# Two-layer hybrid decoder trunk: a re-planned start, three accumulator banks, joined PV groups and a split last output piece

## Chip, core and metric

The kernel runs on one core of a Trainium2 chip. The metric is the device time of one execution in microseconds (us), here the median of three runs. The profile is one further execution, with its own time.

## What is computed

`x` is 256 tokens by 1024 columns, float32. Layer 0 normalises it, projects it once, and splits the columns between a Mamba-2 SSD mixer and a dilated attention mixer of 24 heads; layer 1 is a causal attention of 16 heads. Cut to what matters here:

```python
# layer 0
proj = rms_norm(x, norm_w) @ w_in              # 1024 -> 8208 columns: z, xbc, dt, q, k, v, g
xs, B, C = split(silu(causal_dwconv(xbc)))     # conv of 4 taps per column
y = ssd(xs, softplus(dt + bias), -exp(a_log), B, C) + d_skip * xs
y = rms_norm_per_group(y * silu(z))
q, k = rope(rms_norm(q)), rope(rms_norm(k))    # per head, 24 heads of 64
o = merge_by_softmax([attention(q, k, v, window, dilation) for 3 groups]) * silu(g)
x = x + concat(y, o) @ w_out                   # 1536 -> 1024
# layer 1: with 256 tokens the one block of 256 makes it plain causal attention
q, k, v, g = split(rms_norm(x) @ w_in1)        # 4 x 1024 columns, 16 heads of 64
x = x + (causal_attention(rope(rms_norm(q)), rope(rms_norm(k)), v) * silu(g)) @ w_out1
```

## The kernel before

All weights are brought as 58 tiles of 128 x 2048 float32 (1 MB) in the order of use. `load_split` (line 576) loads a tile in two DMAs of 512 KB into `raw`; ScalarE casts each half to fp32r (`whi`, line 591) and VectorE takes the difference (`wlo`, line 592). Each product of activations and weights is three matmuls (`mm3`, line 667, and `proj_fm`): high by high, high by low, low by high. `raw`, `whi` and `wlo` have three buffers each, so a tile is prepared two ahead of its use.

The first projections (`q2`, `v0`, `k01_0`) read the transposed input `xt_host` (`load_xf`, line 1212, tile names `k` and `mix`), the later ones `xh` and `xl`, which `normalise` (line 1234) writes from the same data once the row norms (`rms`, line 631) are known. Ten matmuls on zeros warm TensorE first (line 1205). One `for` over `ORDER0`, then the output projection (`out_proj`, line 725), then `ORDER1`, then the second `out_proj`, whose `finish` is `store` (line 1319): two halves of 256 columns are added and written out for each piece.

PSUM has eight banks: two under the tag `acc` for projections and six under `x` for everything else (line 566): score tiles, transposes (`x<-cst,...`, `cst` holding the identity), PV sums and broadcasts. Score matmuls (`x<-qkT,qkT`) use 64 of 128 rows and PV matmuls (`x<-p,k`) 64 of 128 columns; two of them run side by side in the halves of the array. `plan.group()` keeps the matmuls of one such group together.

Nothing is issued as it is written. Every call is recorded (`record`, line 240), and `Plan.order` (line 343) lays the recorded operations out on the five engines by a list schedule: among the operations that a table of costs (`price`, line 286) holds to be ready, the one recorded first goes first, buffers being given out as they come free. `choose` (line 445) stays in a half-array shape while it can. `emit` (line 497) then issues all of it; so every profile row has line L504. A changed number in `price`, another count of banks or another position in the recording re-lays the whole program.

Of the kernel before, what the change touches and what calls it, by code (L numbers as in the profile page):

```python
# [20 lines left out]
S = 256  # L21
# [14 lines left out]
NWARM = 10  # L36
# [149 lines left out]
class Plan:  # L186
# [15 lines left out]
    def __init__(self, nc, sbuf, psum):  # L202
        self.nc, self.sbuf, self.psum = nc, sbuf, psum
        self.ops, self.tags, self.groups = [], {}, []
        for e in self.ENGINES:
            setattr(self, e, Recorder(self, e))
# [31 lines left out]


    def record(self, engine, method, args, kw):  # L240
# [45 lines left out]
    def price(self, op, outs, ins):  # L286
# [8 lines left out]
        if e == "pe":  # L295
# [4 lines left out]
            elif lhs.dtype == F32R:  # L300
                c = max(119.5, 0.453 * n + 5)
# [41 lines left out]
    def order(self):  # L343
# [8 lines left out]
        for op in ops:  # L352
            op.left = len(op.preds)
            op.ready = 0.0
            for p in op.preds:
                ops[p].succs.append(op.seq)
# [6 lines left out]
        for op in ops:  # L363
            if not op.left:
                heapq.heappush(waiting[op.engine], (0.0, op.seq))
# [180 lines left out]
def trunk_kernel(ctx: ExitStack, tc: tile.TileContext, x, tiles_host, dtw_host, norms, xt_host, params, bparams, consts, causal_mask, out):  # L546
# [18 lines left out]
    def pst(tag, shape=(P, 512)):  # L565
        tag, bufs = ("acc", 2) if tag == "acc" else ("x", 6)
# [9 lines left out]
    def load_split(between=()):  # L576
# [4 lines left out]
        for h in range(2):  # L581
            sl = slice(1024 * h, 1024 * h + 1024)
# [5 lines left out]
        step = 1024 // n  # L588
        for k in range(0, nk, step):
            sl = slice(k, k + step)  # L590
# [134 lines left out]
    def out_proj(mix, parts, finish, by_column=()):  # L725

        accs, nk = {}, len(mix)
        for k0, n in parts:
# [3 lines left out]
            def run(t, c, k):  # L732
# [4 lines left out]
                mm3(accs[t, c], (h[:, ts_], l[:, ts_]), (wh[:, kk, :], wl[:, kk, :]), k == 0, k == nk - 1)  # L737

            if not last:
                for c in range(2):  # L740
                    for i in range(n // 4):
                        w[c, i] = weights()
                        for t in range(NT):
                            if k0 + i == 0:
                                accs[t, c] = pst("o" if (t, c) == (1, 1) else "acc")
                            for k in range(4):
                                run(t, c, k0 + 4 * i + k)
            else:
                w = {(c, 0): weights() for c in range(2)}
                for t in range(NT):  # L750
                    steps = [(c, k) for k in range(k0, nk) for c in range(2)]
                    for c, k in sorted(steps) if t in by_column else steps:
                        run(t, c, k)
                        if k == nk - 1:
                            finish(t, c, accs[t, c])

# [34 lines left out]
    def small_params():  # L791
        rows = sb([NROWS, P], name="rows")
        sp.dma_start(rows, params)
        tp = pst("t")
        pe.transpose(tp[:, :NROWS], rows, ident[:NROWS, :NROWS])
        dve.tensor_copy(pc, tp[:, :NROWS])
        sp.dma_start(bp, bass.AP(bparams.tensor, bparams.offset, [[0, P], [1, 160]]))
# [18 lines left out]
    def dt_path():  # L816
        sp.dma_start(flat(dtw), dtw_host)
# [226 lines left out]
    def pv(op, pTs, vs, first, last, dilated=False):  # L1044

        with plan.group():
            for kt, (c0, n, l0) in enumerate(((0, 128, 0), (128, 128, 0)) if dilated else ((0, 256, 0), (256, 128, 128))):
                for j in range(2):
                    o = op[64 * j:64 * j + 64, :]
                    o = blocks(o)[:, kt] if dilated else o[:, l0:l0 + n]  # L1050
                    pe.matmul(o, vs[j][kt], pTs[j][:, c0:c0 + n], start=first and kt == 0, stop=last and kt == 1)
# [75 lines left out]
    def dil_pair(pr):  # L1127
        def fn():
            op = pst("o")
            for g in range(3):  # L1130
# [4 lines left out]
                pv(op[:, :S], pTs, vs, g == 0, g == 2, g > 0)  # L1135
# [71 lines left out]
    dve.memset(all1, 1.0)  # L1207
    sp.dma_start(ncol, norms)
# [10 lines left out]
    load_split([lambda: load_xf(1)])  # L1219
    load_xf(2)  # L1220
    load_split([lambda: load_xf(3)])
    sp.dma_start(ident, consts[:, IDN:IDN + P])
    load_split()
    for t in range(NT):
        load_x(t)
    first, normal = Rows(lambda k: entry[k]), Rows(lambda k: (xh[:, k, :], xl[:, k, :]))
# [17 lines left out]
    def switch(n):  # L1244
        if n == FIRST - 2:
            normalise()
        if n == FIRST - 1:
# [55 lines left out]
    def pairs1(c):  # L1303
        def fn():
            for j in range(0, 8, 2):
# [3 lines left out]
                pv(op[:, :S], pTs, [[state[f"V{c}"][t][:, j + i, :] for t in range(NT)] for i in range(2)], True, True)  # L1309
# [9 lines left out]
    def store(t, c, acc):  # L1319
        for h in range(2):  # L1320
            sl = slice(256 * h, 256 * h + 256)
            dve.tensor_tensor(xt[t, c][:, sl], xt[t, c][:, sl], acc[:, sl], ALU.add)
# [42 lines left out]
```

## Time and profile before

| | us |
|---|---|
| median of 3 runs (lowest, highest) | 410.09 (409.61, 410.75) |
| profiled execution, its own time | 411.14 |
| its span, first to last instruction | 409.4 |
| TensorE busy in the span | 399.6 |
| VectorE busy | 319.7 |
| ScalarE busy | 258.3 |
| GpSimd busy | 58.2 |

A row of the timeline gives the start in us, the time it covers, engine, operation, the tiles as out<-in, the shape, and in brackets the idle time before it with what ended that. PE is the matmul side of TensorE. A float32 matmul stands as two records, an fp32r one as one; records overlap, since the next matmul starts while one drains, so the distance of starts is the time that a matmul takes up.

### The profile page before, as it was taken

Reading aid. Unit: us, or ns where it says so; the run is one execution under the profiler, and the core shown is the slowest. Engines: PE = TensorE matmul, PEld = TensorE weight load, DVE = VectorE, ACT = ScalarE, POOL = GpSimd, SP = SyncE. Lnnn points to the kernel's source line nnn. Section 1 sums busy time; section 2 is a strip of 40 time slices with the busy share of each in tenths; the row PEclk is TensorE's granted clock in tenths of the full one; section 3 lists DMA queues with packets and bytes.
Section 4 is the critical chain, followed back from the end, with each engine's and each line's share of the span. In section 5 each row is a group of like instructions: output and inputs, shape, how many; then the busy total and the mean of one; then the engine's idle time right before and its main releaser. Section 6 shows DMA issues by size and latency. Waiting matters only on the chain.

```text
span 409.4 us, 7018 instructions
## 1 busy us (share of the span) xinstructions
PE 399.6 (98%) x2511; PEld 339.2 (83%) x2511; DVE 319.7 (78%) x809; ACT 258.3 (63%) x530; POOL 58.2 (14%) x65
## 2 busy tenths in 40 slices
PE   5999999999999999999999999999999999999996
PEld 5878999999889677778889888888878978879784
DVE  3788999999679999999948794597589756698532
ACT  4778666466356696568677963586569646586610
POOL 0080310000022000334004000002430004500000
PEclk9899999999999999999999999999999999999999
DMA  7997565556636235545518344264741734543002
GB/s 232 379 357 258 193 227 178 163 179 199 203 108 255 96 114 189 171 161 165 165 59 287 117 155 155 83 228 149 251 163 54 252 98 156 177 142 102 2 26 77
DMA packets 22994, 68.82 MB, mean 168 GB/s; under 512 B 4163, under 2 KB 5936, under 8 KB 22960
## 3 DMA queue, kind: packets, MB, share of 16 engines
q1 hardware_dynamic: 22960, 68.39, 50.5%
q8 instruction: 19, 0.31, 0.3%
q14 instruction: 15, 0.12, 0.1%
HBM read 67.28 MB, written 1.10 MB: 167 GB/s over the span
## 4 chain that ended last, share of the span: by engine, by line
PE 87%; DVE 7%; DMA 3%; POOL 1%; ACT 1%; issue 0%; SPq 0%; DVEq 0%
PE acc L504 69%; PE x L504 18%; DVE p L504 3%; DVE wlo L504 2%; DMA raw<-in_tiles_dram 1%; DMA qkT<-cd 1%; DVE k L504 1%; POOL ysq L504 1%; ACT k L504 1%; SPq L504 0%; ACT whi L504 0%; DVE t L504 0%; DVE rq L504 0%; POOL rq L504 0%; DVEq L1361 0%
## 5 line engine op out<-in xcount | busy, mean ns | idle before, releaser
L504 DVE TENSOR_TENSOR wlo<-raw,whi 128x1024 fp32r<-128x1024 f32 x116 | 139.7, 1219 | 24.8 <-ACT whi L504 23.9
L504 ACT CAST whi<-raw 128x1024 fp32r<-128x1024 f32 x116 | 119.5, 1050 | 31.8 <-PE acc L504 21.1
L504 PE MATMUL acc<-xh,whi 128*128 128x256 f32 x288 | 80.4, 279 | 0.0
L504 PE MATMUL acc<-xh,wlo 128*128 128x256 f32 x288 | 80.2, 278 | 0.0
L504 PE MATMUL acc<-xl,whi 128*128 128x256 f32 x288 | 79.9, 277 | 0.0
L504 PE MATMUL acc<-whi,xh 128*128 128x512 f32 x192 | 77.8, 405 | 0.0
L504 PE MATMUL acc<-wlo,xh 128*128 128x512 f32 x192 | 76.5, 399 | 0.0
L504 PE MATMUL acc<-whi,xl 128*128 128x512 f32 x192 | 76.5, 399 | 0.0
L504 PE MATMUL acc<-whi,mix 128*128 128x512 f32 x216 | 70.9, 403 | 2.9 <-ACT whi L504 2.3
L504 PEld LDWEIGHTS acc<-xh,whi 128*128 128x128 f32 x288 | 54.1, 188 | 0.7 <-issue 0.5
L504 PEld LDWEIGHTS acc<-xh,wlo 128*128 128x128 f32 x288 | 54.2, 188 | 0.3 <-issue 0.2
L504 PEld LDWEIGHTS acc<-xl,whi 128*128 128x128 f32 x288 | 54.1, 188 | 0.2
L504 PEld LDWEIGHTS acc<-whi,mix 128*128 128x128 f32 x216 | 41.1, 191 | 12.5 <-ACT whi L504 2.5
L504 PE MATMUL acc<-wlo,mix 128*128 128x512 f32 x108 | 43.1, 401 | 0.5 <-DVE wlo L504 0.5
L504 PEld LDWEIGHTS acc<-whi,xh 128*128 128x128 f32 x192 | 36.3, 189 | 8.6 <-issue 1.5
L504 PEld LDWEIGHTS acc<-wlo,xh 128*128 128x128 f32 x192 | 36.3, 189 | 8.5 <-issue 1.6
L504 PEld LDWEIGHTS acc<-whi,xl 128*128 128x128 f32 x192 | 36.3, 189 | 7.3 <-issue 0.2
L504 POOL TENSOR_TENSOR rq<-rq,nhalf 128x8 f32<-128x8 f32 x20 | 40.1, 2011 | 1.4
L504 ACT COPY k<-acc 128x512 f32<-128x512 f32 x24 | 14.1, 586 | 29.4 <-PE acc L504 29.4
L504 ACT ACTIVATE k<-k 128x512 f32<-128x512 f32 x20 | 12.7, 636 | 21.4 <-DVE k L504 21.4
L504 PEld LDWEIGHTS acc<-wlo,mix 128*128 128x128 f32 x108 | 20.7, 192 | 5.1 <-DVE wlo L504 1.0
L504 DVE TENSOR_REDUCE rq<-k 128x8 f32<-128x512 f32 x20 | 13.6, 682 | 11.5 <-ACT k L504 11.3
(150 smaller groups left out, 541.4 us busy)
## 6 DMA issues: line engine op xcount, KB each, us to landing
raw<-in_tiles_dram SPq DMA_DIRECT2D x116, 512.0 KB, 4.8
k<-in_x_dram SPq DMA_DIRECT2D x8, 256.0 KB, 6.4
qkT<-cd SPq DMA_DIRECT2D x4, 512.0 KB, 4.7
k<-in_xt_dram SPq DMA_DIRECT2D x4, 256.0 KB, 6.8
out_dram<-k SPq DMA_DIRECT2D x8, 128.0 KB, 1.8
cst<-in_consts_dram SPq DMA_DIRECT2D x1, 640.0 KB, 5.7
cst<-in_causal_mask_dram SPq DMA_DIRECT2D x1, 192.0 KB, 3.1
cst<-in_consts_dram SPq DMA_DIRECT2D x2, 64.0 KB, 5.8
```

The costliest lines, as they stand in the source:

```text
L504: getattr(eng[op.engine], op.method)(*[real(a) for a in op.args], **{k: real(v) for k, v in op.kw.items()})
```

## The change

The first weight tile is loaded and prepared in pieces of 512, 512 and 1024 columns; a small activation on ScalarE loads its table at the start; eleven warming matmuls instead of ten. The parameter rows, the rope tables and `bp` are loaded directly behind the first three tiles, and two weight tiles more are recorded ahead of the loads of `x`; those, `dtw` and the large constants get an earliest planning time. Three `acc` banks and five `x` banks. The PV matmuls of the three dilation groups of a head pair form one group. The last piece of the second output projection has two accumulators of 256 columns. The planner's price of an fp32r matmul changes.

```diff
-NWARM = 10
+NWARM = 11
@@ Plan
+    def later(self, n):        # recorded priorities inside are put back by n
+    def not_before(self, ns):  # operations inside are not planned ahead of ns
...
-        op.prio = op.seq
+        op.prio = op.seq + self.delay
+        op.ready = self.earliest
...
-                c = max(119.5, 0.453 * n + 5)
+                c = max(114.5, 0.447 * n)
@@ pst
-        tag, bufs = ("acc", 2) if tag == "acc" else ("x", 6)
+        tag, bufs = ("acc", 3) if tag == "acc" else ("x", 5)
@@ load_split
-        for h in range(2):
-            sl = slice(1024 * h, 1024 * h + 1024)
+        pieces = (512, 512, 1024) if i == 0 else (1024, 1024)
+        c = 0
+        for size in pieces:
+            sl = slice(c, c + size)
+            c += size
             sp.dma_start(flat(raw)[:, sl], tiles_host[i, :, sl])
...
-        step = 1024 // n
-        for k in range(0, nk, step):
-            sl = slice(k, k + step)
+        k = 0
+        for size in pieces:
+            sl = slice(k, k + size // n)
+            k += size // n
             act.copy(hi[:, sl, :], raw[:, sl, :])
@@ out_proj(mix, parts, finish, by_column=(), halves=False)
+                            split_up = halves and (t, c) == (NT - 1, 1)
+                                if split_up:
+                                    half_accs += [pst("o", (P, 256)) for _ in range(2)]
...
+                for hf in range(2 if halves else 0):
+                    for k in range(k0, nk):
+                        run_halves(k, hf)       # run(...) on 256 columns of the weights
+                    finish(NT - 1, 1, half_accs[hf], hf)
@@ small_params
         sp.dma_start(rows, params)
+        sp.dma_start(cst[:, ROPE:], consts[:, ROPE:])
+        sp.dma_start(bp, bass.AP(bparams.tensor, bparams.offset, [[0, P], [1, 160]]))
...
@@ dt_path
-        sp.dma_start(flat(dtw), dtw_host)
+        with plan.not_before(24000.0):
+            sp.dma_start(flat(dtw), dtw_host)
@@ pv: its "with plan.group():" goes
@@ dil_pair
+            todo = []
             for g in range(3):
...
-                pv(op[:, :S], pTs, vs, g == 0, g == 2, g > 0)
+                todo.append((pTs, vs, g == 0, g == 2, g > 0))
+            with plan.group():
+                for args in todo:
+                    pv(op[:, :S], *args)
@@ trunk_kernel, the start
     dve.memset(all1, 1.0)
+    act.activation(sb([P, 8], name="junk"), nhalf, AF.Copy, scale=1.0)
...
-    load_split([lambda: load_xf(1)])
+    load_split([lambda: None, lambda: load_xf(1)])
     load_xf(2)
     load_split([lambda: load_xf(3)])
     sp.dma_start(ident, consts[:, IDN:IDN + P])
+    with plan.later(60):
+        small_params()
     load_split()
-    for t in range(NT):
-        load_x(t)
-    for t in range(NT):
-        rms(t, first)
-    sp.dma_start(cst[:, IDN + P:], consts[:, IDN + P:])
-    small_params()
-    sp.dma_start(cst[:, :IDN], consts[:, :IDN])
+    load_split()
+    with plan.not_before(11300.0):
+        for t in range(NT):
+            load_x(t)
+    with plan.later(120):
+        for t in range(NT):
+            rms(t, first)
...                             # in switch(FIRST - 2), behind normalise():
+            with plan.not_before(21000.0):
+                sp.dma_start(cst[:, :IDN], consts[:, :IDN])
@@ the second output projection; store adds and writes one half when it gets one
-    out_proj([state["mix1", k] for k in range(8)], PARTS1, store, (1,))
+    out_proj([state["mix1", k] for k in range(8)], PARTS1, store, (1,), True)
```

SyncE's queue at the start of the program, before; `k` from `in_xt` is the transposed input, `k` from `in_x` the plain one, `raw` a weight tile, `rows` and `bp` the parameters:

```order
L504 DMA k_1_83<-in_xt_dram 128x512
L504 DMA raw_127<-in_tiles_dram 128x1024
L504 DMA k_2_84<-in_xt_dram 128x512
...
L504 DMA raw_129<-in_tiles_dram 128x1024 x2
L504 DMA k_5_87<-in_x_dram 128x512
L504 DMA k_6_88<-in_x_dram 128x512
L504 DMA k_7_89<-in_x_dram 128x512
L504 DMA k_8_90<-in_x_dram 128x512
L504 DMA cst_0_65<-in_consts_dram 128x128
```

And the same stretch of the queue now:

```order
L519 DMA k_1_83<-in_xt_dram 128x512
L519 DMA raw_127<-in_tiles_dram 128x512 x2
L519 DMA k_2_84<-in_xt_dram 128x512
...
L519 DMA raw_129<-in_tiles_dram 128x1024 x2
L519 DMA rows_0_136<-in_params_dram 93x128
L519 DMA cst_0_65<-in_consts_dram 128x128
L519 DMA bp_0_72<-in_bparams_dram 128x160
L519 DMA raw_127<-in_tiles_dram 128x1024 x2
L519 DMA k_5_87<-in_x_dram 128x512
```

The first tile comes in three pieces, and the plain `x` stands behind the parameters and a fourth weight tile.

TensorE where the first projection ends and the second one, `v0`, begins, before:

```order
L504 MATMUL acc_148<-whi_131,mix_116 128x512
L504 MATMUL acc_148<-wlo_134,mix_116 128x512
L504 MATMUL acc_148<-whi_131,mix_118 128x512
L504 MATMUL x_98<-cst_0_65,rows_0_142 128x93
L504 MATMUL acc_147<-whi_132,mix_103 128x512
```

And now:

```order
L519 MATMUL acc_148<-whi_131,mix_116 128x512
L519 MATMUL acc_148<-wlo_134,mix_116 128x512
L519 MATMUL acc_148<-whi_131,mix_118 128x512
L519 MATMUL acc_149<-whi_132,mix_103 128x512
L519 MATMUL acc_149<-wlo_135,mix_103 128x512
```

`v0` begins in a bank of its own, where it had to take the first one over from the first projection.

TensorE in the scores of the first half of layer 1, before (twelve score matmuls end with the first two rows):

```order
L504 MATMUL x_98<-qkT_152,qkT_149 128x256
L504 MATMUL x_99<-qkT_152,qkT_149 128x256
L504 MATMUL acc_148<-whi_131,xh_0_63 128x512
L504 MATMUL x_102<-qkT_152,qkT_149 128x128
L504 MATMUL x_97<-qkT_152,qkT_149 128x128
L504 MATMUL x_102<-qkT_152,qkT_149 128x256
L504 MATMUL x_97<-qkT_152,qkT_149 128x256
L504 MATMUL acc_148<-wlo_134,xh_0_63 128x512
```

And now (eight end with the first two rows):

```order
L519 MATMUL x_100<-qkT_153,qkT_150 128x256
L519 MATMUL x_101<-qkT_153,qkT_150 128x256
L519 MATMUL acc_147<-whi_131,xh_0_63 128x512
L519 MATMUL x_99<-qkT_153,qkT_150 128x128
L519 MATMUL x_97<-qkT_153,qkT_150 128x128
L519 MATMUL x_99<-qkT_153,qkT_150 128x256
L519 MATMUL x_97<-qkT_153,qkT_150 128x256
L519 MATMUL acc_147<-wlo_134,xh_0_63 128x512
L519 MATMUL x_98<-qkT_153,qkT_150 128x128
```

The sixteen score matmuls of these four head pairs stand in three runs instead of two. Over the whole program the score matmuls stand in 15 runs instead of 10, the PV matmuls in 16 instead of 17.

## Rows read from the trace of the kernel before

**Rows 1.** The page's first part: engine, busy us, share, instructions.

```profile
PE 399.6 (98%) x2511; PEld 339.2 (83%) x2511; DVE 319.7 (78%) x809; ACT 258.3 (63%) x530; POOL 58.2 (14%) x65
```

**Rows 2.** Busy time by stage: stretch, length, busy us (instructions) by engine, clock, DMA.

```profile
33.00:105.00 72.00, 72.00 (x571) 69.30 (x570) 67.91 (x122) 46.18 (x64) 4.67 (x4) 1.00 0.60 195
123.50:145.00 21.50, 20.98 (x167) 17.41 (x167) 21.50 (x68) 14.75 (x37) 3.06 (x3) 1.00 0.44 160
145.00:207.00 62.00, 61.31 (x336) 47.76 (x336) 56.98 (x177) 43.08 (x105) 11.96 (x10) 1.00 0.51 166
```

**Rows 3.** Timeline of the first 8 us: warming matmuls and the table load.

```profile
1.43 4.64 PE L504 MATMUL x<-k 128*128 128x128 f32 x20 [1.43 <-DVE k L504]
3.85 1.28 ACT L504 ACT_TABLE_LOAD   x1 [3.85 <-DMA k<-in_xt_dram]
```

**Rows 4.** Timeline from 7 to 17 us: first weights and first matmuls.

```profile
7.23 1.04 ACT L504 CAST whi<-raw 128x1024 fp32r<-128x1024 f32 x1 [1.17 <-DMA raw<-in_tiles_dram]
...
8.32 0.73 PE L504 MATMUL acc<-whi,mix 128*128 128x512 f32 x2 [2.25 <-ACT whi L504]
...
9.18 1.05 ACT L504 CAST whi<-raw 128x1024 fp32r<-128x1024 f32 x1
...
9.59 0.50 PE L504 MATMUL acc<-wlo,mix 128*128 128x512 f32 x1 [0.53 <-DVE wlo L504]
...
10.26 1.23 DVE L504 TENSOR_TENSOR wlo<-raw,whi 128x1024 fp32r<-128x1024 f32 x1
...
15.88 0.39 PE L504 MATMUL acc<-wlo,mix 128*128 128x512 f32 x1
16.10 0.62 PE L504 MATMUL acc<-whi,mix 128*128 128x512 f32 x2
```

**Rows 5.** TensorE by stretch: busy us (matmuls), granted clock, DMA share, GB/s.

```profile
6.70:10.00 3.30, 1.15 (x4) 1.00 1.02 337
10.10:13.40 3.30, 3.30 (x9) 0.50 1.03 386
```

**Rows 6.** All engines while the first input tile lands; the last number is GB/s.

```profile
2.00:3.20 1.20, 1.20 (x8) 1.20 (x7) 0.00 (x0) 0.00 (x0) 0.00 (x0) 1.00 0.68 208
```

**Rows 7.** Timeline where the second projection begins.

```profile
21.78 0.24 PE L504 MATMUL x<-cst,rows 93*128 93x93 f32 x1
...
22.67 0.50 PE L504 MATMUL acc<-whi,mix 128*128 128x512 f32 x1 [0.65 <-ACT k L504]
```

**Rows 8.** Timeline of TensorE in the scores of layer 1.

```profile
304.99 2.24 PE L504 MATMUL x<-qkT,qkT 64*128 64x128 f32 x24
307.16 0.50 PE L504 MATMUL acc<-whi,xh 128*128 128x512 f32 x1
307.58 0.93 PE L504 MATMUL x<-qkT,qkT 64*128 64x128 f32 x8
```

**Rows 9.** Timeline of TensorE in the PV products of layer 1.

```profile
324.88 1.52 PE L504 MATMUL x<-p,k 128*64 128x256 f32 x16
...
327.29 0.48 PE L504 MATMUL acc<-whi,xl 128*128 128x512 f32 x1
327.70 0.87 PE L504 MATMUL x<-p,k 128*64 128x256 f32 x8
```

**Rows 10.** Timeline of TensorE from 134 to 178 us: its idle times.

```profile
136.55 0.86 PE L504 MATMUL x<-p,k 128*64 128x256 f32 x6 [0.50 <-DVE p L504]
...
176.71 1.12 PE L504 MATMUL x<-k,all 128*128 128x512 f32 x2 [0.60 <-DVE k L504]
```

**Rows 11.** GpSimd from 24 to 34 us: the powers for the first norms.

```profile
25.81 5.16 POOL L504 TENSOR_TENSOR rq<-rq,nhalf 128x8 f32<-128x8 f32 x2
```

**Rows 12.** Timeline of the end: last matmul, last additions, output DMAs.

```profile
401.82 5.11 SPq L504 DMA_DIRECT2D out_dram<-k  x6
...
405.25 0.39 PE L504 MATMUL x<-whi,mix 128*128 128x512 f32 x1
405.68 0.75 DVE L504 TENSOR_TENSOR k<-k,x 128x256 f32<-128x256 f32 x2 [1.97 <-PE x L504]
```

More of the change, by code (lines that the diff above doesn't have):

```diff
@@ L237, in group @@
         self.groups.append([op.seq for op in self.ops[first:] if op.engine == "pe"])
+    @contextmanager
+    def later(self, n):
+        self.delay += n
+        yield
+        self.delay -= n
+    @contextmanager
+    def not_before(self, ns):
+        self.earliest = ns
+        yield
+        self.earliest = 0.0
     def record(self, engine, method, args, kw):
@@ L364, in order @@
             if not op.left:
-                heapq.heappush(waiting[op.engine], (0.0, op.seq))
+                heapq.heappush(waiting[op.engine], (op.ready, op.seq))
         todo, now, order = len(ops), 0.0, []
@@ L730, in out_proj, with run @@
             last = k0 + n == nk
-            def run(t, c, k):
+            def run(t, c, k, cols=slice(0, 512)):
                 h, l = mix[k]
@@ L736, in run, with run_halves @@
                 kk = (k - k0) % 4
-                mm3(accs[t, c], (h[:, ts_], l[:, ts_]), (wh[:, kk, :], wl[:, kk, :]), k == 0, k == nk - 1)
+                mm3(accs[t, c], (h[:, ts_], l[:, ts_]), (wh[:, kk, cols], wl[:, kk, cols]), k == 0, k == nk - 1)
+            def run_halves(k, hf):
+                accs[NT - 1, 1] = half_accs[hf]
+                run(NT - 1, 1, k, slice(256 * hf, 256 * hf + 256))
             if not last:
@@ L743, in out_proj @@
                         for t in range(NT):
+                            split_up = halves and (t, c) == (NT - 1, 1)
                             if k0 + i == 0:
-                                accs[t, c] = pst("o" if (t, c) == (1, 1) else "acc")
-                            for k in range(4):
-                                run(t, c, k0 + 4 * i + k)
+                                if split_up:
+                                    half_accs += [pst("o", (P, 256)) for _ in range(2)]
+                                else:
+                                    accs[t, c] = pst("o" if (t, c) == (1, 1) else "acc")
+                            for k in range(k0 + 4 * i, k0 + 4 * i + 4):
+                                if split_up:
+                                    for hf in range(2):
+                                        run_halves(k, hf)
+                                else:
+                                    run(t, c, k)
             else:
@@ L752, in out_proj @@
                     for c, k in sorted(steps) if t in by_column else steps:
+                        if halves and (t, c) == (NT - 1, 1):
+                            continue
                         run(t, c, k)
@@ L1044, in pv @@
     def pv(op, pTs, vs, first, last, dilated=False):
[L1046 to L1051, printed above, removed]
+        for kt, (c0, n, l0) in enumerate(((0, 128, 0), (128, 128, 0)) if dilated else ((0, 256, 0), (256, 128, 128))):
+            for j in range(2):
+                o = op[64 * j:64 * j + 64, :]
+                o = blocks(o)[:, kt] if dilated else o[:, l0:l0 + n]
+                pe.matmul(o, vs[j][kt], pTs[j][:, c0:c0 + n], start=first and kt == 0, stop=last and kt == 1)
     def v_chunk(rows, perm=False):
@@ L1308, in fn @@
                 op = pst("o")
-                pv(op[:, :S], pTs, [[state[f"V{c}"][t][:, j + i, :] for t in range(NT)] for i in range(2)], True, True)
+                with plan.group():
+                  pv(op[:, :S], pTs, [[state[f"V{c}"][t][:, j + i, :] for t in range(NT)] for i in range(2)], True, True)
                 state["mix1", 4 * c + j // 2] = gate_out(op[:, :S], state[f"G{c}"][j // 4][:, (j // 2) % 2, :])
@@ L1317, in trunk_kernel, with store @@
     ov = out[0].rearrange("(t p) d -> p t d", p=P)
-    def store(t, c, acc):
-        for h in range(2):
+    def store(t, c, acc, half=None):
+        for h in range(2) if half is None else (half,):
             sl = slice(256 * h, 256 * h + 256)
-            dve.tensor_tensor(xt[t, c][:, sl], xt[t, c][:, sl], acc[:, sl], ALU.add)
+            dve.tensor_tensor(xt[t, c][:, sl], xt[t, c][:, sl], acc[:, sl] if half is None else acc, ALU.add)
             sp.dma_start(ov[:, t, 512 * c + 256 * h:512 * c + 256 * h + 256], xt[t, c][:, sl])
-    out_proj([state["mix1", k] for k in range(8)], PARTS1, store, (1,))
+    out_proj([state["mix1", k] for k in range(8)], PARTS1, store, (1,), True)
     plan.emit(tc)
```

10 lines of the change are left out of this document (5 added, 5 removed).

## Prediction

> **What bounds the kernel now.** I read the page's busy times first: the reader should see that the matmul side of TensorE is busy 399.6 of 409.4 us and VectorE 319.7 [rows 1]. So nearly all of the span is matmul time, and only three things can move it: idle time of TensorE, the slow clock, and the time that the matmuls themselves take up. The stage table comes next. From 33 to 105 us TensorE has no idle time while VectorE is busy 67.91 of 72; from 123.5 to 145 VectorE is busy all 21.5, and from 145 to 207 for 56.98 of 62 [rows 2]. There the two engines are nearly level, and time won on TensorE ahead of that stage counts only if VectorE can be as early. Then the timeline of the start: ten warming matmuls from 1.43 to 6.07 [rows 3], idle until the first weights are cast, 2.25 us, then 0.53 us for the first `wlo` [rows 4]. The clock column shows the price: full from 6.7 to 10.0, where TensorE is busy 1.15 of 3.3, and half (1.2 GHz) from 10.1 to 13.4 [rows 5]. The other idle times are short: 0.65 us behind 21.78 for an `acc` bank [rows 7], 0.50 and 0.60 for VectorE [rows 10]. Last the end: the final matmul starts at 405.25, the two additions begin at 405.68, and the last of their DMAs is issued by 406.93 [rows 12].
>
> The sum is made against the profiled execution: 411.14 us, of which 409.4 are span and 1.74 lie around it. It stands 1.05 above the median of 410.09; I take the same difference off the median.
>
> **First weights, table, warming.** Eleven warming matmuls at 4.64 / 10 = 0.46 us end at 1.43 + 5.1 = 6.5 [rows 3]. The first input tile is there at 3.85 [rows 3]. The first piece is 256 KB behind it: at the 208 GB/s of that stretch [rows 6] 1.26 us, at the 155 GB/s that 512 KB between 3.85 and 7.23 make [rows 3, 4] 1.7 us, so it lands at 5.1 to 5.55. Its cast is half of 1.04 us [rows 4], with no table load of 1.28 us ahead of it: done by 6.1. The warming, not the weights, then holds the first matmul: 6.5 instead of 8.32. The second piece is in by 7.23 as before, for no more bytes lie ahead of it; its cast and its `wlo` (half of 1.23) end near 8.4, and the twelve matmuls of these two pieces, 0.22 to 0.23 apart (15.88 to 16.10 in [rows 4]; 0.227 taken), are done before 10. What is late next is the third piece, which the early pieces do not hasten: its cast ends at 10.23 and its `wlo` at 11.49 [rows 4]. In the new order the 15th matmul needs that `wlo`. So the 24th starts at 11.5 + 9 x 0.227 = 13.55 where it started at 16.10 [rows 4], which is 2.55 us earlier if the clock stays full. (Before, 8 matmuls at half clock lost 8 x 0.2 = 1.6 us of this.) One DMA issue more stands ahead of the third piece; I take 2.3 and keep 0.5 to 2.55 as bounds. Of the table load by itself I expect nothing: ScalarE is idle for 1.17 us behind it anyway [rows 4].
>
> The rule that speaks on this is in the Trainium skill, "TensorE: Matmul & The Clock Gate", section "HAM oscillation — how this bites in real kernels": the clock goes back to its lower level only when the engine lies idle in one long unbroken gap. The rows differ: two short gaps, 2.25 and 0.53 us, were followed by half clock. By the page the new waits, each shorter than those, could not cost the clock, and the first rival below would have no chance; by the rows it keeps one.
>
> **Three accumulator banks.** `v0` no longer takes over the bank of `q2`, whose square stood behind three squares of `x` on ScalarE. The 0.65 us [rows 7] and the restart behind it go: 0.7. What is late next there are the norms: `x` now lands behind 1 MB more of weights, and the two powers for the first norms take 5.16 us on GpSimd [rows 11] before the transposes of `q2` may start. By my count they come just in time, so I cost them at nothing; if the cover is gone it is up to 1 us.
>
> **Moved loads.** The parameters, rope tables, `dtw` and constants are the same bytes in another order; weights are two tiles ahead all the time, so nothing on TensorE waits for them: 0. Their DMA issues stand in SyncE's queue between weight tiles, and a tile held up there would show as a wait for `whi`.
>
> **The order in the SSD stage.** Between the cumulative sum and the first PV group stand 11.2 us of TensorE work instead of 12.2, but the following groups lie about 3 us apart where two pairs lay together, and the broadcast before the norm of the second half comes 6.4 instead of 4.4 us behind its sums (matmuls counted in the two orders, times their distances). So the waits of 0.50 and 0.60 us for VectorE [rows 10] should go: 1.1. Nothing of the trace shows the new waits there; the bounds are 1.6 gained (with the loose starts around these waits) and 1.6 lost.
>
> **Joined groups.** Within one run of half-array matmuls a further group costs (2.24 - 0.93) / 2 = 0.655 us in the scores, but alone 0.93, and the full matmul ahead of a run waits 307.58 - 307.16 = 0.42 instead of 0.23 us [rows 8]: a run more costs 0.275 + 0.19 = 0.47. For PV it is 0.87 - (1.52 - 0.87) = 0.22 and 0.41 - 0.23 = 0.18, together 0.40 [rows 9]. The new order has 15 runs of scores where it had 10, and 16 of PV where it had 17. The joining does save a run in each half of layer 1, but the dilated pairs were already run in two stretches and still are. So this costs 5 x 0.47 - 0.40 = 1.95 at most; runs of only 128-column matmuls should be cheaper, and I take 1.6, with 0.8 to 2.0 as bounds.
>
> This is the rule that speaks against the change: the Trainium skill, "TensorEngine Tiling (Array Packing)", section "Key Properties", says that a change of tiling mode drains TensorE. The rows agree with about 0.4 us for each run. It has no price; without this term the sum would be -4.5.
>
> **The end.** The last 24 half-width matmuls take as long as 12 full ones. Only one addition and one DMA issue are left behind the last matmul instead of two: half of 0.75 us, and a little of the second issue [rows 12]: 0.4, between 0.3 and 0.6.
>
> Sum: -2.3 - 0.7 - 1.1 + 1.6 - 0.4 = -2.9 us: 408.2 for the profiled execution, 407.2 for the median.
>
> **The rivals.**
> 1. *The clock falls again.* After 9 us TensorE waits twice, near 10 for the cast and near 11 for `wlo`. If the next stretch is again granted half, up to 1.6 us are lost: 408.8. For it: the rows of before. Against it: the twelve early matmuls make the stretch before far busier than 1.15 of 3.3 us. 0.11.
> 2. *The early pieces do not land early.* If the engines divide among the outstanding DMAs so that the first piece lands near 7.2, the gap behind the warming and the half clock stay, and the start gives 0.5: -2.9 + 1.8, 409.0. For it: the first 512 KB came at only 155 GB/s. 0.08.
> 3. *The lead is given back.* VectorE has no idle time from 123.5 to 145 and 5 us from 145 to 207 [rows 2]. If its chain there does not start earlier, what is won before it is lost there, and only the end and the runs behind 207 us remain: -0.4 + 0.2, 409.9. Against it: VectorE waits for TensorE at the head of that stage. 0.08.
> 4. *Five x banks are too few, slower.* Each of the twelve head pairs takes x banks for its scores, transposes and sum. A wait for a bank costs 0.65 where one showed [rows 7]. From the fifth such wait on the gain is gone; at eight it is -2.9 + 5.2, 412.4. Against it: the planner gives out the five banks and orders around them. 0.07.
>
> **How the numbers follow.** My forecast has 0.66. Within it the time lies between 405.5 and 408.5. About 0.3% (1.2 us) is what a measurement of this kernel can tell from no change: 408.9 and 411.3. Faster by more: 0.66 less a little for its upper edge, and half of rival 1, with some of 2: 0.74. Within: the rest of 1 and 2, and 3: 0.19. Slower: 0.07. The range reaches from 405.4, with the waits in the SSD stage and the runs at their better bounds, to 409.3, which takes in 1 and 2 and leaves out 3 and 4.
>
> **What would show it.** Right: first weight matmul near 6.5 and the 24th near 13.6, clock 1.00 from 6.7 on; no idle TensorE near 19, where `v0` begins; fewer than two waits for VectorE between 110 and 180; single runs of four score matmuls in layer 1, each with 0.9 us; one addition behind the last matmul. Wrong: a half-clock row behind 10 us; idle TensorE between 30 and 35 us for the transposes of `q2`; or TensorE waiting in many places for ScalarE's copies out of x banks, which would make it slower.

## The result: slower, and the profile after

The changed kernel takes 413.48 us (median of 4 runs, 413.05 to 413.76) where the kernel before took 410.42 beside it: ratio 1.0074, 95% interval 1.005 to 1.0097. The forecast was 407.2, with a range up to 409.3. The profiled execution took 413.3 us, with a span of 411.5.

Most rows that the prediction named came out as it said. The page's busy times come first. TensorE is busy 4.5 us longer than in [rows 1], and no other engine has changed by much.

```profile
PE 404.1 (98%) x2537; PEld 341.7 (83%) x2537; DVE 319.9 (78%) x810; ACT 259.5 (63%) x532; POOL 58.5 (14%) x65
```

The start, from the timeline. The first weights are cast at 5.64, the first weight matmul starts at 6.32 (6.5 forecast; it waits 0.45 us for the cast, so the weights hold it and not the warming, as the prediction had it), the wait for the `wlo` of the third piece is where it was expected, and the last row is the 24th matmul: 13.90 instead of 16.10 [rows 4], 2.2 us earlier (2.3 forecast).

```profile
1.44 4.43 PE L519 MATMUL x<-k 128*128 128x128 f32 x22 [1.44 <-DVE k L519]
...
5.64 0.62 ACT L519 CAST whi<-raw 128x512 fp32r<-128x512 f32 x1 [0.87 <-DMA raw<-in_tiles_dram]
...
6.32 0.73 PE L519 MATMUL acc<-whi,mix 128*128 128x512 f32 x2 [0.45 <-ACT whi L519]
...
11.72 0.50 PE L519 MATMUL acc<-wlo,mix 128*128 128x512 f32 x1 [0.53 <-DVE wlo L519]
...
13.90 0.39 PE L519 MATMUL acc<-whi,mix 128*128 128x512 f32 x1
```

TensorE by stretch at the start (busy, matmuls, granted clock, DMA share, GB/s): the clock column reads 1.00 in both, and 15 matmuls fall into the 4 us of the second where 9 filled the 3.3 us of [rows 5], so the half clock is gone.

```profile
5.90:10.00 4.10, 3.38 (x11) 1.00 0.97 379
10.00:14.00 4.00, 3.47 (x15) 1.00 1.04 403
```

At the head of `v0` the bracket of [rows 7] is gone, and by stage (as in [rows 2], where 123.5 to 207 us held 1.2 us of idle TensorE) the waits of the SSD stage are gone too.

```profile
17.78 0.48 PE L519 MATMUL acc<-wlo,mix 128*128 128x512 f32 x1
18.10 0.63 PE L519 MATMUL acc<-whi,mix 128*128 128x512 f32 x2
```

```profile
33.00:105.00 72.00, 71.31 (x563) 69.05 (x562) 65.87 (x122) 45.24 (x65) 6.02 (x4) 1.00 0.57 191
123.50:145.00 21.50, 21.50 (x158) 16.49 (x157) 21.20 (x75) 15.17 (x39) 2.44 (x3) 1.00 0.42 143
145.00:207.00 62.00, 62.00 (x334) 48.78 (x333) 59.07 (x171) 43.75 (x98) 10.12 (x10) 1.00 0.53 171
```

The end: the last matmul starts 3.45 us ahead of the end of the span (4.15 before, [rows 12]), with one addition behind it.

```profile
407.38 1.77 SPq L519 DMA_DIRECT2D out_dram<-k  x2
...
408.05 0.28 PE L519 MATMUL x<-whi,mix 128*128 128x256 f32 x1
408.36 0.42 DVE L519 TENSOR_TENSOR k<-k,x 128x256 f32<-128x256 f32 x1 [1.01 <-PE x L519]
```

The scores of layer 1 run as one stretch and two single groups, the singles at 0.93 us as in [rows 8].

```profile
307.17 1.58 PE L519 MATMUL x<-qkT,qkT 64*128 64x128 f32 x16
...
309.11 0.93 PE L519 MATMUL x<-qkT,qkT 64*128 64x128 f32 x8
...
310.40 0.93 PE L519 MATMUL x<-qkT,qkT 64*128 64x128 f32 x8
```

Two things were not forecast. One is small, two new waits for VectorE:

```profile
53.70 0.66 PE L519 MATMUL x<-cst,k 128*128 128x128 f32 x4 [0.69 <-DVE k L519]
...
270.84 0.66 PE L519 MATMUL x<-cst,k 128*128 128x128 f32 x4 [0.83 <-DVE k L519]
```

The other is not a wait at all. In the stretch from 82 to 100 us TensorE does nothing but matmuls of 256 columns, back to back, in both kernels and at full clock, with no idle time. Before, 161 of them lie at least in part in these 18 us (first fence); after, 156 (second). By their starts it is 159 and 154.

```profile
82.00:100.00 18.00, 18.00 (x161) 1.00 0.57 183
```

```profile
82.00:100.00 18.00, 18.00 (x156) 1.00 0.66 218
```

The groups of instructions tell the same (count, busy us, mean ns of one), of before and then of after: the mean of one goes up by 2 to 5 ns.

```profile
L504 PE MATMUL acc<-xh,whi 128*128 128x256 f32 x288 | 80.4, 279 | 0.0
L504 PE MATMUL acc<-xh,wlo 128*128 128x256 f32 x288 | 80.2, 278 | 0.0
L504 PE MATMUL acc<-xl,whi 128*128 128x256 f32 x288 | 79.9, 277 | 0.0
```

```profile
L519 PE MATMUL acc<-xh,wlo 128*128 128x256 f32 x288 | 81.2, 282 | 0.0
L519 PE MATMUL acc<-xl,whi 128*128 128x256 f32 x288 | 81.1, 282 | 0.0
L519 PE MATMUL acc<-xh,whi 128*128 128x256 f32 x288 | 80.9, 281 | 0.0
```

From the starts in the trace, pauses left out (distances under 160, and between 200 and 300 ns), the mean distance from one matmul to the next is:

| matmuls | before | after | difference x count |
|---|---|---|---|
| 256 columns, `xh`/`xl` with weights | 114.3 ns (848) | 118.0 ns (850) | +3.1 us |
| 512 columns, `xh`/`xl` with weights | 230.4 ns (521) | 233.4 ns (510) | +1.5 us |
| 512 columns, `mix` with weights | 228.0 ns (349) | 227.9 ns (320) | 0 |

That is 4.6 us on products that the change doesn't touch. Why the third row stays is the clue on which the experiments turn.

### The profile page after: what moved, and what is told of

It reads as the page before. It is cut to its first block, busy times and chain, and to the rows that moved or that the text cites. A ratio compares the mean times of both kernels' runs of the same rounds, so it can differ in the third digit from the quotient of the medians.

```text
span 411.5 us, 7072 instructions
## 1 busy us (share of the span) xinstructions
PE 404.1 (98%) x2537; PEld 341.7 (83%) x2537; DVE 319.9 (78%) x810; ACT 259.5 (63%) x532; POOL 58.5 (14%) x65
## 4 chain that ended last, share of the span: by engine, by line
PE 91%; DVE 4%; DMA 2%; POOL 1%; issue 1%; ACT 1%; SPq 1%; DVEq 0%
PE acc L519 71%; PE x L519 19%; DMA raw<-in_tiles_dram 2%; DVE wlo L519 1%; DVE k L519 1%; POOL rq L519 1%; DVE xl L519 1%; SPq L519 1%; DVE rq L519 0%; ACT xh L519 0%; ACT whi L519 0%; ACT k L519 0%; DVE t L519 0%; DVEq L519 0%
## 5 line engine op out<-in xcount | busy, mean ns | idle before, releaser
L519 DVE TENSOR_TENSOR wlo<-raw,whi 128x1024 fp32r<-128x1024 f32 (+1 forms) x117 | 140.2, 1212 | 17.5 <-ACT whi L519 17.2
L519 ACT CAST whi<-raw 128x1024 fp32r<-128x1024 f32 (+1 forms) x117 | 119.6, 1043 | 31.7 <-PE acc L519 22.1
L519 PE MATMUL acc<-xh,wlo 128*128 128x256 f32 x288 | 81.2, 282 | 0.0
L519 PE MATMUL acc<-xl,whi 128*128 128x256 f32 x288 | 81.1, 282 | 0.0
L519 PE MATMUL acc<-wlo,xh 128*128 128x512 f32 x192 | 77.6, 404 | 0.0
L519 PE MATMUL acc<-whi,xl 128*128 128x512 f32 x192 | 77.4, 403 | 0.0
L519 POOL TENSOR_TENSOR rq<-rq,nhalf 128x8 f32<-128x8 f32 x20 | 36.6, 1831 | 1.5
```

The lines of the kernel that those rows point to most:

```text
L519: getattr(eng[op.engine], op.method)(*[real(a) for a in op.args], **{k: real(v) for k, v in op.kw.items()})
```

## The experiments

Two explanations were open. The tiles lie in a partition in the order in which they are first used, and the new activation at the start writes a new tile of 32 bytes ahead of `mix`, `raw`, `whi`, `wlo`: all of these moved by 32 bytes, `xh` and `xl` did not. Or the order and the banks are to blame.

**Four runs on place and banks.** `a_junk64` makes the tile 64 bytes, `b_shift32` puts an unused 32-byte tile into the kernel before, `a_acc2` and `b_acc3` change the banks alone (with another count of banks the planner re-lays the program).

```diff
-    act.activation(sb([P, 8], name="junk"), nhalf, AF.Copy, scale=1.0)
+    act.activation(sb([P, 16], name="junk")[:, :8], nhalf, AF.Copy, scale=1.0)   # a_junk64
+    plan.tag("pad", 1, 8, F32, "sb")                       # b_shift32, behind memset(all1)
-        ... ("acc", 3) if tag == "acc" else ("x", 5)
+        ... ("acc", 2) if tag == "acc" else ("x", 6)       # a_acc2; b_acc3 the reverse
```

> The changed kernel with its new 8-column tile (32 bytes a partition) made 64 bytes, so that every tile behind it (mix, raw, whi, wlo, qkT, p and the small ones) starts on a multiple of 64 bytes again, as in the kernel before; the order of the instructions is the same word for word. Theory A (the 32-byte shift makes each matmul that reads xh or xl with whi or wlo wait longer): the distance between 256-column matmuls falls from 118 to 113 ns, 864 of them, and of the 512-column ones with xh, xl from 232-235 to 229-231, 576 of them; 3.6 to 4.3 us and 1.2 to 2 us, so about 407.5 to 408.5 us, 0.99 of the kernel before. Rival B (the new order of the matmuls, or the bank that an accumulator has, sets the distance): 118 ns stays and the time stays at 413.4.

> The kernel before with nothing but an unused tile of 32 bytes ahead of mix, so that mix and all tiles behind it start 32 bytes off a multiple of 64. Theory A: 256-column matmuls go from 113 to 117-118 ns, the time from 410.3 to 414.5-416. Rival B: no change, 410.3 within 0.3%.

> The changed kernel with two acc and six x banks as before, everything else kept, the 32-byte shift too. Theory A: the distance stays at 118 ns and the time goes up by the 0.7 us of the acc wait at v0 or stays, 413.4 to 414.2. Rival B in its form 'three acc banks cost': 113 ns again, about 408.

> The kernel before with three acc and five x banks, nothing else. Theory A: the distance stays at 113 ns; the acc wait of 0.65 us at v0 goes, 409.3 to 410.3. Rival 'five x banks are too few': 411 or more. Rival B in its form 'three acc banks cost': 118 ns, 414.

| | time, us | ratio (95%) | 256 columns, ns | 512 columns, ns |
|---|---|---|---|---|
| `b_shift32` | 415.13 | 1.0121 (1.0102 to 1.0139) | 117.9 | 233.3 |
| `a_junk64` | 413.73 | 1.0094 (1.0075 to 1.0114) | 118.8 | 232.6 |
| `a_acc2` | 416.64 | 1.0162 (1.0146 to 1.0178) | 118.2 | 233.4 |
| `b_acc3` | 415.97 | 1.0145 (1.013 to 1.016) | 116.8 | 230.3 |

`b_shift32` alone shows the whole effect: 32 unused bytes, the same instructions in the same order, 1.2% slower. But `a_junk64` misses: with every tile on a multiple of 64 again it is as slow as the changed kernel, so "multiple of 64" is not the rule. And in `b_acc3`, with nothing moved, the 256-column distance went up to 116.8; looked at stream by stream it stands at two levels, 113.3 and 117.8, as it does in the kernel before (there mostly 113.3). `b_acc3` also has four new waits for VectorE, 4.2 us together, where three waits of before are gone (0.65, 0.50 and 0.60 us). These 2.4 us and the 2.1 us of the 256-column distance (2.5 ns x 848) make 4.5 of the 5.9 us that it loses; the rest is not traced. The four waits:

```profile
51.94 0.66 PE L504 MATMUL x<-cst,k 128*128 128x128 f32 x4 [1.27 <-DVE k L504]
...
193.78 0.63 PE L504 MATMUL x<-cst,k 128*128 128x128 f32 x4 [0.92 <-DVE k L504]
...
268.77 0.66 PE L504 MATMUL x<-cst,k 128*128 128x128 f32 x4 [0.98 <-DVE k L504]
...
272.96 0.66 PE L504 MATMUL x<-cst,k 128*128 128x128 f32 x4 [1.02 <-DVE k L504]
```

`a_acc2`, at the same distances as the changed kernel, is 3.2 us slower than it by the medians: in that order three banks instead of two are worth far more than the 0.7 us forecast. Its waits behind the start (the first one the changed kernel has too):

```profile
54.80 0.66 PE L519 MATMUL x<-cst,k 128*128 128x128 f32 x4 [0.69 <-DVE k L519]
...
60.32 0.36 PE L519 MATMUL acc<-xh,whi 128*128 128x256 f32 x1 [1.14 <-DVE k L519]
...
139.80 0.66 PE L519 MATMUL x<-cst,k 128*128 128x128 f32 x4 [1.07 <-DVE k L519]
140.82 0.48 PE L519 MATMUL acc<-whi,xh 128*128 128x512 f32 x1 [0.37 <-DVE k L519]
...
151.92 0.51 PE L519 MATMUL acc<-whi,xh 128*128 128x512 f32 x1 [0.68 <-ACT k L519]
```

**A map of the distance.** New theory: the stationary and the moving slice are read at the same time, and what counts is where they lie to each other. `m_map` measures the second half of this on TensorE alone; distances in bytes are given modulo 256, as the remainder after division by 256. Its core, cut to the 256-column streams, is

```python
for o in OFF:                       # o: start of the weight slice, in elements of 4 bytes
    for n in (1, 2, 3):
        other(n)                    # n plain fp32 matmuls in between
        for i in range(8):          # stationary wh/wl from o + 256 i, moving xh/xl from 256 i
            mm3(a[:, :256], (wh[:, st], wl[:, st]), (xh[:, mv], xl[:, mv]), i == 0, i == 7)
```

> TensorE alone, on tiles of zeros, nothing of the reference computed: streams of 24 fp32r matmuls of 256 columns (stationary a 128-column slice of wh or wl, moving 256 columns of xh or xl, in the kernel's order) and of 12 of 512 columns (stationary from xh, xl, moving from wh, wl), after one, two or three plain fp32 matmuls, with the start of the w slice moved in steps of 16 bytes against that of the x slice, 0 to 480 bytes and 512, 1024, 2048, 4096 and 8192 (each also 64 more). Theory C (the distance of matmuls depends on where the stationary and the moving slice lie to each other, since both are read at the same time): the medians fall into levels by this distance, about 113 ns at 64 bytes, 117 at 96, 119 at 128 (256 columns), 229, 232 and 232 (512 columns), with the same at equal remainders. Rival D (another engine's traffic, or the order around it, makes the levels): one level, 113 ns and 227 to 229 ns, at every distance.

Two streams of it from the timeline, both with the weight slice at 64 bytes (modulo 256). In the first, 22 distances between 60.25 and 62.74 make 113.2 ns; in the second, between 63.64 and 66.23, 117.7.

```profile
59.68 0.60 PE L519 MATMUL x<-k 128*128 128x128 f32 x4
60.04 0.37 PE L519 MATMUL acc<-xh,wh 128*128 128x256 f32 x1
60.25 0.28 PE L519 MATMUL acc<-xl,wh 128*128 128x256 f32 x1
...
62.74 0.28 PE L519 MATMUL acc<-xh,wl 128*128 128x256 f32 x1
62.86 0.83 PE L519 MATMUL x<-k 128*128 128x128 f32 x6
63.44 0.36 PE L519 MATMUL acc<-xh,wh 128*128 128x256 f32 x1
63.64 0.28 PE L519 MATMUL acc<-xl,wh 128*128 128x256 f32 x1
...
66.23 0.28 PE L519 MATMUL acc<-xh,wl 128*128 128x256 f32 x1
```

All of it, mean ns from the seventh distance of each stream on:

```
start of w minus start of x,     256 columns, stationary w     512 columns, moving w
modulo 256 bytes                 after 1, 2, 3 fp32 matmuls    after 1, 2
  0                              120.0  120.0  120.0           227.4  226.6
 32                              118.4  118.4  118.2           233.6  233.8
 64                              113.4  113.4  117.8           229.0  228.8
 96                              117.2  117.4  118.5           233.6  233.8
128                              118.4  118.8  118.4           233.6  230.6
160                              119.8  119.8  120.2           234.2  234.2
192                              117.8  117.8  117.8           233.8  233.2
224                              116.9  116.8  116.6           233.6  233.8
256 (same as 0)                  120.0  120.0  120.0           226.6  226.6
320 (same as 64)                 113.4  113.4  117.8           229.0  228.8
```

At 512, 1024, 2048, 4096 and 8192 bytes the rows for 0 and 64 repeat within 0.3 ns, but for the single 227.4; 16, 48, 80 and 112 bytes lie between 117.6 and 120.3, and between 231.2 and 233.4. Theory C holds in what it says of the distance, and D falls: no other engine does anything here, and the means of the real kernels so far lie within 1.5 ns of the table. That the two reads get in each other's way is the likely reason, but no run shows it. By the sizes of the tiles `whi` starts 106,048 bytes behind `xh` before (64 modulo 256), 32 more after (96), 64 more in `a_junk64` (128). `mix` moved along with the weights, 49,152 bytes apart (0), so its 512-column products kept their 228 (227 in the map), the third row of the first table. The new half-width matmuls of the last piece, `mix` with 256 columns at distance 0, stand at 120 ns.

**Which of the two levels.** `m_state` holds the distance at 64 and varies what stands between two streams.

```python
KINDS = [("f", n) for n in range(9)] + [("t", n) for n in (1, 2, 3)]             # plain fp32, 128 and 64 columns
KINDS += [("r", n) for n in (1, 2, 3, 4)] + [("h", n) for n in (2, 4, 6)]        # fp32r, half-row
SEQ = [KINDS[(a * s) % 19] for s in (1, 4, 7, 11, 13) for a in range(19)]
```

> TensorE alone on zeros, nothing of the reference computed: the stream of 24 fp32r matmuls of 256 columns with its stationary slice always 64 bytes (modulo 256) behind the moving one, the distance at which two levels were seen, after 0 to 8 plain fp32 matmuls of 128 columns, 1 to 3 of 64 columns, 1 to 4 fp32r ones of 128 columns, or 2, 4 and 6 half-row ones, each five times in different neighbourhoods. Theory E (what stands directly ahead of a stream sets its level): the same kind and count gives the same level each time, 113.3 or 117.8. Rival F (the level is carried on from what was before, or is chance): one kind gives both levels.

Neither theory holds as written. The same kind gave both levels, but not by chance: with one, three, five or seven plain fp32 matmul instructions of 128 columns between, the level changed from that of the stream before, 20 times of 20; with two, four, six or eight it stayed, 20 of 20. The other kinds mostly follow the same rule, four of them not every time (two fp32 of 64 columns, three and four fp32r, four half-row). So the level is carried on, and an odd number of plain fp32 instructions flips it. That fits whole stretches of the kernels standing at 113.3 or at 117.8 ns, and changing sides when the order is re-laid (95 matmuls from 311.1 us on stand at 113.5 ns before, 95 from 314.6 us on at 117.8 in `b_acc3`). It is not the whole rule: `a_opt` below has the instructions in the same order as `a_shift0`, word for word, and its level flips all the same. What in the engine holds this state, no run shows.

**The change without its tile.** `a_shift0` lets the early activation write a tile that exists already, so that all tiles lie as before. `a_start` has the changed start alone, also with the tiles as before.

```diff
-    act.activation(sb([P, 8], name="junk"), nhalf, AF.Copy, scale=1.0)
+    act.activation(nw4, nhalf, AF.Copy, scale=1.0)        # a_shift0; a_start too, with two acc banks,
                                                           # old price, old pv groups, no halves
```

> The changed kernel with the new tile left out (the early table-loading activation writes nw4, a tile that is there already), so that every tile lies where it lay in the kernel before. Theory C: 512-column matmuls with xh, xl fall from 233 to 230 ns (576 of them, 1.7 us) and 256-column ones lie at the two levels 113 and 118 of the kernel before, in stretches: 0 to 4 us of the 864; so 408 to 411.7 us. Rival B (order and banks alone): 118 ns and 413.4 stay.

> The changed start alone (pieces, table, warming, order of loads), with the tiles where they lay before; two acc banks, the old price, one group for each PV call, the last piece not split. The sum of the prediction for the start is 2.3 us: 407.7. Theory C adds 0 to 3.5 us by how much of the 256-column work stands at 118 ns instead of 113: 407.7 to 411.2. Rival: another order of steps after the start brings new waits, 412 or more.

`a_shift0`: 408.75 us, ratio 0.9972 (0.9955 to 0.999), distances 114.1 and 230.3 ns. One 32-byte tile is 4.7 us by the medians (1.0074 against 0.9972, 4.2 us by the ratios), the whole way from faster to slower. In the stretch of 82 to 100 us:

```profile
82.00:100.00 18.00, 18.00 (x162) 1.00 0.68 221
```

`a_start`: 410.69 us, ratio 1.0022 (1.0005 to 1.004), distances 114.6 and 230.5. The early start by itself wins nothing. In its trace the 24th matmul starts at 15.02 us, 1.1 us earlier than before, and the 256-column matmuls begin at 44.07 instead of 46.00; but at its third group of transposes TensorE waits 1.56 us for VectorE, where the kernel before did not wait, and two shorter waits follow. The row of before, and then those of `a_start`:

```profile
52.61 0.66 PE L504 MATMUL x<-cst,k 128*128 128x128 f32 x4
```

```profile
52.97 0.66 PE L519 MATMUL x<-cst,k 128*128 128x128 f32 x4 [1.56 <-DVE k L519]
...
137.71 0.66 PE L519 MATMUL x<-cst,k 128*128 128x128 f32 x4 [0.63 <-DVE k L519]
138.74 0.48 PE L519 MATMUL acc<-whi,xh 128*128 128x512 f32 x1 [0.37 <-DVE k L519]
```

**Parts of the change on that ground.** `a_opt` moves the 512-column weight tiles that meet `xh` and `xl` to distance 0; `a_s0_nohalf` leaves out the split of the last piece; `a_s0_nopv` groups the PV matmuls as before.

```diff
+        off = 48 if n == 512 and i >= 6 and "out" not in specs[i][0] else 0     # a_opt, load_split
+        hi, lo = (sb([P, 2112], F32R, tag=tag, bufs=NW)[:, off:off + 2048].rearrange(...) for tag in ("whi", "wlo"))
-    out_proj([state["mix1", k] for k in range(8)], PARTS1, store, (1,), True)
+    out_proj([state["mix1", k] for k in range(8)], PARTS1, store, (1,))         # a_s0_nohalf
-            with plan.group():                                                  # a_s0_nopv, dil_pair
-                for args in todo:
-                    pv(op[:, :S], *args)
+                pv(op[:, :S], pTs, vs, g == 0, g == 2, g > 0)                   # in the loop over g; pv groups itself
```

> The changed kernel without the new tile (as a_shift0), and with the 512-column weight tiles that meet xh and xl placed 192 bytes further into buffers of 8448 bytes, so that they lie at distance 0 modulo 256 to xh and xl, while the 256-column ones stay at distance 64; the order of the instructions is that of a_shift0 word for word. Theory C: 576 matmuls go from 230.3 to 226.7 ns, 2.1 us off a_shift0: 406.7 us, 0.992 of the kernel before. Rival: that distance does not matter in the kernel, where VectorE, ScalarE and the DMAs read and write beside it: 408.7 us.

> a_shift0 without the split of the last output piece. By the prediction's term for the end the split is worth 0.4 us: 409.2 us. By the map the 48 half-width matmuls stand at distance 0 and 120 ns, so the split pays 48 x 6.7 = 0.3 us of that back: 408.8 us.

> a_shift0 with the PV matmuls grouped as in the kernel before (one group for each call of pv). By the prediction the joined groups are worth little either way, runs of half-array matmuls at 0.15 us each: 408 to 409.5 us. Rival: the joined groups hold back the PV matmuls until the last operand is there, and single groups are faster by a microsecond or more, under 407.7.

`a_opt`: 409.65 us, ratio 0.9986 (0.9973 to 0.9999), a miss. The 512-column products of layer 1 fell towards what the map says (229.5 to 228 ns), those of the SSD stage, with other matmuls in between, did not (231.4 both times), and the level of the 256-column streams from 118 us on flipped: 117.8 instead of about 113.6 in nearly all of them, with not one instruction more or less between them. On the mean, 850 x 1.6 ns = 1.4 us are lost and 510 x 0.9 ns = 0.5 us won, the 0.9 us that it is slower than `a_shift0` by the medians (the intervals of the two ratios overlap).

`a_s0_nohalf`: 409.19 us, ratio 0.9971 (0.9958 to 0.9984), the same as with the split; its value is below what these runs resolve.

`a_s0_nopv`: 407.54 us, ratio 0.9931 (0.9912 to 0.995), faster than both kernels. That it comes within 0.3 us of the forecast is luck: the forecast was for the joined groups. Without them 1.2 us are won by the medians, 1.7 by the ratios. TensorE's order is another from about 203 us on; the PV matmuls still stand in 16 runs, the scores in 14 instead of 15. 0.83 us is a wait that `a_shift0` has in the second half of the first output projection, where VectorE reaches the addition for the transposes too late, and `a_s0_nopv` does not have:

```profile
268.46 0.66 PE L519 MATMUL x<-cst,k 128*128 128x128 f32 x4 [0.83 <-DVE k L519]
```

**The distance, or the address itself.** In the kernels so far `mix` and the weights moved, and `xh` and `xl` stayed. `a_all32` moves all tiles by 32 bytes together, `a_junk256` keeps the new tile but makes it 256 bytes.

```diff
+    plan.tag("pad", 1, 8, F32, "sb")                      # a_all32: a_shift0 with this ahead of xh
-    act.activation(sb([P, 8], name="junk"), nhalf, AF.Copy, scale=1.0)
+    act.activation(sb([P, 64], name="junk")[:, :8], nhalf, AF.Copy, scale=1.0)  # a_junk256
```

> a_shift0 with an unused 32-byte tile ahead of xh, the first tile: everything, xh and xl as well, starts 32 bytes off a multiple of 64 as in the changed kernel, while the distance between xh, xl and the weight tiles stays 64 bytes (modulo 256); order word for word as in a_shift0. Theory C (only the distance between the two slices counts): 113/118 and 230 ns as in a_shift0, 408.7 us. Rival G (the start address itself counts, a multiple of 64 is fast): 117 to 119 and 233 ns, 413 us.

> The changed kernel with its new tile made 256 bytes a partition (64 columns, of which 8 are written), nothing else: the weight tiles lie 256 bytes further than in the kernel before, at the same distance modulo 256 to xh and xl; order as in the changed kernel. Theory C with a period of 256 bytes: as a_shift0, 408.7 us. Rival: any move of the weight tiles costs, 413 us.

`a_all32`: 408.71 us, ratio 0.9967 (0.9958 to 0.9976); `a_junk256`: 408.65, ratio 0.997 (0.9958 to 0.9981). The distances are 114.1 and 230.3 ns in both. Rival G falls: in `a_all32` every tile starts 32 bytes off a multiple of 64, as in the changed kernel, and nothing is lost. `a_junk256` is the changed kernel but for the size of one scratch tile, and is 4.8 us faster by the medians. In 82 to 100 us, `a_all32`:

```profile
82.00:100.00 18.00, 18.00 (x162) 1.00 0.69 219
```

## Why the prediction was wrong

The step that failed is in "First weights, table, warming": "Of the table load by itself I expect nothing". I priced the activation and what it waits for, and not the tile that it writes. That tile moved the weights from 64 to 96 bytes (modulo 256) against `xh` and `xl`, and 848 and 521 matmuls became 3.7 and 3.0 ns slower. The sum had no term for the distance of a full matmul; it took it from the trace of before as if it were fixed. Without the tile the change measures 408.75, inside the range; no rival was near the true cause. Why a distance of 96 bytes is slower than one of 64 stays open.

The rest of the sum was nearer than -1.2 against -2.9 makes it look. Profiled execution against profiled execution, as the sum was made, `a_shift0` takes 408.95 us and the kernel before 411.14, a gain of 2.2. But the profiled execution of before stood 1.05 above its median and that of `a_shift0` 0.2, so taking the same difference off the median put the forecast 0.85 us lower than the two executions bear out; single executions of one kernel scatter by one to two us.

By its own steps:

- *Start, -2.3.* Right in the rows: 2.2 us earlier at the 24th matmul, clock 1.00, rivals 1 and 2 absent. In `a_acc2`, with the same start, rival 1 did come: half clock from 9.1 to 12.5 us. As a term of the time the start is not worth 2.3 by itself: in `a_start` most of the lead goes to a wait for VectorE, earlier than rival 3 had it, at 53 us.
- *Banks, -0.7.* The wait at `v0` is gone, and the third bank is worth 3.2 us in the new order (`a_acc2`); in the kernel before, re-laid for it and with the level of the streams against it, it costs 5.9 (`b_acc3`, ratio 1.0145). A term for one part of a re-planned program is not a property of that part. Rival 4 did not occur: no row of TensorE in the changed kernel waits for a release of an `x` bank.
- *SSD waits, -1.1.* Gone as forecast, but waits of 0.69 and 0.83 us came at 53.70 and 270.84, which the sum had not.
- *Joined groups, +1.6 with the runs of scores.* Single groups of scores cost the 0.93 us forecast. For PV the number of runs was not the cost: it is 16 with the joining and without it, in layer 1 too, where the prediction gave the joining a run less in each half. The joining costs 1.2 us (`a_shift0` against `a_s0_nopv`), 0.83 of it as one wait for VectorE; that it holds the PV matmuls back, as the rival of that run says, is not shown by itself.
- *End, -0.4.* Right in the rows: 0.7 us less behind the last matmul, and 48 x 6 ns = 0.3 us more for half-width matmuls at 120 ns. No effect on the time could be measured.
- *Range.* Its lower end, 405.4, is lower than the two bounds named for it give: 407.2 - 0.5 - 0.8 = 405.9. Nothing hangs on it.

So -2.9 us was not the sum of terms that each proved right: with its tile out of the way the change gives -1.2, and -2.5 when PV is grouped as before.

## What to carry to other kernels

A tile that is put ahead of others changes where they lie to the tiles in front of it; in a stream of matmuls that showed here in the distance of starts and not as a wait, so compare that distance in a stretch without idle time before looking for waits. Padding the scratch tile to 256 bytes cost nothing here (`a_junk256`). To lay the operands out on purpose, measure the few distances first: weights minus activations, 64 bytes was the best for 256-column fp32r streams, 0 for 512 columns. Then measure the whole kernel: `a_opt`, laid out by such a map, lost 0.9 us by the medians. With a planner that re-lays everything, take the parts of a change back one at a time, with the tiles held in place.

## What the hardware showed that was not expected

- The distance of two fp32r matmuls of 256 columns is 113.3 to 120.3 ns, and of 512 columns 226.6 to 234.2, by the start of the weight slice minus that of the activation slice, with a period of 256 bytes (`m_map`; the weights are stationary with 256 columns and moving with 512).
- At a distance of 64 bytes there are two levels, 113.3 and 117.8 ns, carried on from stream to stream and flipped by an odd number of plain fp32 matmul instructions between them (20 of 20, and 20 of 20 unchanged for even numbers; `m_state`). In `a_opt` the level flipped without such a change, so more than this number sets it.
- The Trainium skill, "TensorE: Matmul & The Clock Gate", section "Step-by-step: what each phase is for", says that loading the next weights takes no read bandwidth from the running matmul, since TensorE has two independent read ports. If that were all, the place of the two operands to each other should not matter; the runs differ: with the same kind of stream and only the distance changed, a 256-column matmul took 113.4 or 120.0 ns (`m_map`).
- In the changed kernel waits of 0.45, 0.31 and 0.53 us, with TensorE busy 3.38 of 4.1 us ahead of the last, left the clock at 1.00, where 1.15 of 3.3 us had been followed by half clock [rows 5]. In `a_acc2` waits of 0.34 and 0.95 us, busy 1.91 of 3.2 us, were followed by it too (first row below); in `a_start` one of 1.30 us, busy 2.79 of 4.1, was not.
- The clock column can miss half clock. In `b_shift32` it reads 1.00 from 10.0 to 13.4 us (second row), but as many matmuls fit into this stretch as into the one of `a_acc2`, and they start 0.43 us apart, as those of before at half clock did; at full clock 17 fit into 3.4 us (`a_acc2` from 12.5 us on). So check it by the distance of starts.

```profile
9.10:12.50 3.40, 3.40 (x9) 0.51 1.04 370
10.00:13.40 3.40, 3.40 (x9) 1.00 0.98 366
```
